# Decayed cumulative sum of a matrix product: group 14 by seven block products instead of eight, slots 34 to 243 ordered by a list scheduler

## The chip, the cores and the metric

The kernel runs on one core of a Trainium2 chip. The metric is the device time of one execution in microseconds (us); three executions of the kernel before gave a median of 905.18 us (904.9 to 905.23). The engines are named as in the profile: PE (TensorE, matmuls), PEld (its weight loads), DVE (VectorE), ACT (ScalarE), POOL (GpSimd) and SP (SyncE, which here only issues DMAs).

## The reference

```python
B, S, D = x.shape                 # 16, 2048, 1024, float32
xw = x @ w                        # w: 1024 x 1024
out[:, 0, :] = xw[:, 0, :]
for t in range(1, S):
    out[:, t, :] = decay[None, :] * out[:, t - 1, :] + xw[:, t, :]
```

A product of a 32768 x 1024 matrix with a 1024 x 1024 one, and behind it, in each of the 16 batches and 1024 columns, a first-order recurrence along 2048 time steps.

## The kernel before, in words

**Data.** Time is cut into 64 chunks of 512 steps; four chunks make a batch and two neighbouring chunks a group (31 whole groups, 0 to 30, and chunks 62 and 63 one by one at the end). x comes by DMAs from POOL's queue that turn fp32 into bf16 (`load`, "L", four to a chunk, ring `xb` of 3). DVE transposes the chunk in 32 x 32 blocks (`turn`, "T", ring `xw` of 2), ACT copies it in two halves into the form that the matmul reads (`part`, "X" and "Y", 128 x 2048 bf16 each, ring `xt` of 5). w lies in SBUF as bf16 (`wsb`).

**Slots.** A slot is one tile: a group (1024 time steps) times 128 output columns n of 8. `slots` lists them group by group: 248 slots with two chunks, then 16 with one chunk. PE works a slot as 16 matmuls 128 x 128 x 512 (8 blocks k of the contraction times 2 chunks) into one PSUM tile `ps`, from a ring of three (two PSUM banks each, called a slot's bank below); the last slots take `spare` too. Slot 112 is the first of group 14, slot 244 is the fifth of group 30.

**The recurrence of a tile** (class `Tile`) goes in one of two ways. *Alone*: DVE scans all 1024 steps from PSUM (`S`, `run`, line 228). *Paired*, which halves the scan: ACT copies `ps` to SBUF (`copy`, "p", line 185) and multiplies the steps of one parity by the decay (`odd`, "g", line 170, into a buffer `h` of four); `zero` ("z") sets the element before the first; POOL adds them (`join`, "j", line 205); DVE scans the 512 pair sums with the squared decay (`S`, line 210); ACT multiplies the results by the decay (`even`, "h"), and POOL adds that to the other parity (`fill`, "c", line 253). `save` ("k") keeps the last step for the next group of the batch. In the slots in question every fourth tile (n % 4 == 3) is alone and the rest is paired. The copy lies in `xs` (ring of 3), the result in `so` (ring of 4).

**Leaving.** DVE transposes the tile into `ot` (`back`, "B", line 265, ring of 4); four tiles fill one `ot` (a lump), and SP's queue stores it with four DMAs (line 289).

**Order.** Each engine takes its instructions in program order. The order is written by hand as letters and slots in `agenda` for slots 0 to 33 and the last 20; for the slots between, `usual` and `later` give the same pattern in each group (two tables of lead slots say when T, X and Y of a chunk come). In the tail (`agenda` -20 and on), flips change which tiles are alone.

Of the kernel before, what the change touches and what calls it, by code (L numbers as in the profile page):

```python
# [25 lines left out]
def kernel(  # L26
# [41 lines left out]
    CR = CH // NQ  # L68

# [24 lines left out]
    def ot_tile(nj):  # L94
        return ring(sb, "ot", 4, [128, nj, CR])

# [22 lines left out]
    def part(c, copy, m0, m1, j0=0, j1=NJ):  # L119
        if c not in xt_of:  # L120
            xt_of[c] = ring(sb, "xt", 5, [128, M, 2, TL], BF16)
        src = xw_of[c][:, m0:m1, j0:j1].rearrange("p m j i e -> p m e (j i)")
        pin(copy(out=xt_of[c][:, m0:m1, :, j0 * P:j1 * P], in_=src))  # L123
# [17 lines left out]
    class Tile:  # L141
# [3 lines left out]
        def __init__(self, g, n, ps, outlets):  # L145
            self.b, self.t0 = chunks[g[0]]
            self.T = TL * len(g)
            self.n, self.ps, self.outlets = n, ps, outlets
            self.paired = n % R != R - 1
            if len(tiles) in flips or len(tiles) - len(slots) in flips:  # L150
                self.paired = not self.paired
            self.turn = len(tiles)
            self.lot = sum(t.paired for t in tiles)
            self.prev = None if self.t0 == 0 else last[n]
            if self.t0 + self.T < S:
                last[n] = const.tile([128, 1], FP32, name=f"keep{n}", bufs=2)
                self.keep = last[n]
            else:
                self.keep = None

        @property
        def so(self):
            if not hasattr(self, "held"):
                self.held = sb.tile([128, 2 * TL + 2], FP32, name=f"so{self.turn % 4}")
            return self.held

        def decayed(self, src, h=None):
            if h is None:
                h = ring(sb, "h", 4, [128, TL])[:, 0:self.T // 2]
            pin(nc.scalar.activation(  # L170
                out=h, in_=src, func=mybir.ActivationFunctionType.Copy,
                scale=dec[:, self.n:self.n + 1]))
            return h
# [8 lines left out]
        def copy(self):  # L182
            self.xs = sb.tile([128, 2 * TL], FP32, name=f"xs{self.lot % 3}")[:, 0:self.T]
            for t, ps in self.parts():
                pin(nc.scalar.copy(out=self.xs[:, t:t + ps.shape[1]], in_=ps))  # L185

        def odd(self):
            self.g = ring(sb, "h", 4, [128, TL])[:, 0:self.T // 2]
            for t, ps in self.parts():
                size = ps.shape[1]  # L190
                self.decayed(ps[:, 0:size:2], self.g[:, t // 2:(t + size) // 2])

# [3 lines left out]

        def zero(self):
            if self.prev is None:
                pin(nc.gpsimd.memset(self.so[:, 1:2], 0.0))  # L199
            else:  # L200
                pin(nc.scalar.copy(out=self.so[:, 1:2], in_=self.prev))  # L201

        def join(self):
            odds = self.xs[:, 1:self.T:2]
            pin(nc.gpsimd.tensor_tensor(out=odds, in0=self.g, in1=odds, op=ALU.add))  # L205

        def scan(self):
            T, n, so = self.T, self.n, self.so
            if self.paired:
                pin(nc.vector.tensor_tensor_scan(  # L210
                    out=so[:, 3:T + 2:2],
                    data0=squares[-1][:, n:n + 1].to_broadcast([128, T // 2]),
                    data1=self.xs[:, 1:T:2],
                    initial=0.0 if self.prev is None else self.prev,
                    op0=ALU.mult,
                    op1=ALU.add,
                ))
            else:
                for t, ps in self.parts():
                    self.run(ps, t, ps.shape[1])  # L220

        def run(self, ps, t, size):
            n, so = self.n, self.so
            if t:
                before = so[:, t + 1:t + 2]
            else:
                before = 0.0 if self.prev is None else self.prev
# [13 lines left out]
        def complete(self):  # L241
            if self.paired:
                self.even()
                self.fill()
            if self.keep is not None:
                self.save()

        def even(self):
            self.h = self.decayed(self.so[:, 1:self.T + 1:2])

        def fill(self):
            T = self.T
            pin(nc.gpsimd.tensor_tensor(  # L253
                out=self.so[:, 2:T + 2:2], in0=self.h, in1=self.xs[:, 0:T:2], op=ALU.add))

        def save(self):
            pin(nc.scalar.copy(out=self.keep, in_=self.so[:, self.T + 1:self.T + 2]))  # L257
# [15 lines left out]
    class Outlet:  # L273


        def __init__(self, ns, nj, half=0, queues=(nc.sync,), pieces=1):
# [3 lines left out]
            self.ot = ot_tile(nj)  # L280
# [135 lines left out]
    def turn_and_load(c):  # L416
# [61 lines left out]
        21: "p20 g20 L S18 X8 j20 B17 B19",  # L478
        22: "L h18 p21 c18 B16 k18 g21 B18 Y8 z20 L j21 S20",
        23: "p22 z21 z22 S21 L h20 g22 T9 c20 h21",  # L480
        24: "k21 k20 j22 S23 X9 L c21 Y9 B20 L",
        25: "B23 k23 p24 B21 g24 z24 j24 S22 z25",
        26: "p25 T10 k22 h22 g25 c22 S24 X10 j25",
        27: "B22 p26 S25 g26 z26 Y10 j26",
# [28 lines left out]
    later = {}  # L513
    begun = {"T": 12, "X": 11, "Y": 11}
    for c in range(5, nch):
        first = c // 2 * K
        ahead = (7, 6, 4) if c % 2 else (11, 10, 8)
        for letter, a in zip("TXY", ahead):
            if c >= begun[letter]:
                later.setdefault(first - a, []).append(f"{letter}{c}")  # L520

    def usual(s):
        paired = [t.paired for t in tiles]
        do = [f"P{s}"] if paired[s] else []
        if paired[s - 1]:
            do.append(f"S{s - 1}")
        if not paired[s]:
            do.append(f"S{s}")
        do.append(f"C{s - 1}")
        if paired[s - 2]:  # L530
            do.append(f"B{s - 2}")
        if not paired[s - 1]:
            do.append(f"B{s - 1}")
        return do + later.get(s, []) + ["L"] * (2 if len(loads) > NQ else 1)

    def rest(s):
        do = [f"S{s - 1}"] if tiles[s - 1].paired else []
        do.append(f"C{s - 1}")
        if tiles[s - 2].paired:
            do.append(f"B{s - 2}")  # L540
        return do + [f"B{s - 1}"] + later.get(s, []) + ["L"] * len(loads)

# [3 lines left out]

    perform(agenda[-99].split())
    spares = [spare] + [ring(psp, "spare1", 1, [128, TL])]
    for step, (g, n) in enumerate(slots):
        T = TL * len(g)  # L550
        left = step - len(slots)
        if n % R == 0:
            ns, nj = range(n, n + R), T // P
            outlets = [Outlet(ns, nj)]
# [54 lines left out]
        do = agenda.get(step, agenda.get(left) if left >= -20 else None)  # L609
        if do is None:  # L610
            do = usual(step)
        else:
            do = do.split()
            if left == -20:
                do = rest(step) + do
        perform(do)
# [29 lines left out]
```

## Time and profile before

| What | Value |
|---|---|
| median of three runs | 905.18 us (904.9 to 905.23) |
| profiled execution, its own time | 905.68 us |
| span of the profiled execution | 903.9 us |
| granted TensorE clock, mean | 0.999 |
| DMA, mean | 227 GB/s |
| store of `ot`, issue to landing, median | 10.9 us |
| load of `xb`, issue to landing, median | 7.9 us |

The profile is of one execution. Rows of groups give a line, an engine and an operation, the tile written and the tiles read, then the count, the busy time, the mean length of one in ns, and the idle time of that engine just before them with what ended it. A length holds the pipeline's fill, so back to back the operations start somewhat closer together than their length. In a timeline a row gives start and length in us. In the chain of waits a row gives start and length of a piece.

### The profile page before, as it was taken

Reading aid. Unit: us, or ns where it says so; the run is one execution under the profiler, and the core shown is the slowest. Engines: PE = TensorE matmul, PEld = TensorE weight load, DVE = VectorE, ACT = ScalarE, POOL = GpSimd, SP = SyncE. Lnnn points to the kernel's source line nnn. Section 1 sums busy time; section 2 is a strip of 40 time slices with the busy share of each in tenths; the row PEclk is TensorE's granted clock in tenths of the full one; section 3 lists DMA queues with packets and bytes.
Section 4 is the critical chain, followed back from the end, with each engine's and each line's share of the span. In section 5 each row is a group of like instructions: output and inputs, shape, how many; then the busy total and the mean of one; then the engine's idle time right before and its main releaser. Section 6 shows DMA issues by size and latency. Waiting matters only on the chain.

```text
span 903.9 us, 12113 instructions
## 1 busy us (share of the span) xinstructions
PE 896.4 (99%) x4217; PEld 412.7 (46%) x4217; DVE 825.5 (91%) x628; ACT 686.3 (76%) x957; POOL 656.7 (73%) x755
## 2 busy tenths in 40 slices
PE   8999999999999999999999999999999999999997
PEld 5544444444444444444444444444444444444444
DVE  4999998999999999999998999999999999999997
ACT  4899967777877877877778778778777787787742
POOL 7978678777767768677677677777777776776632
PEclk9999999999999999999999999999999999999999
DMA  9999999999999999999999999999999999999868
GB/s 186 190 215 215 226 256 217 215 237 236 254 242 260 243 251 257 248 237 226 224 237 229 224 229 229 230 224 229 231 227 228 233 232 222 226 233 211 176 143 235
DMA packets 402542, 204.77 MB, mean 227 GB/s; under 512 B 8752, under 2 KB 401456, under 8 KB 402480
## 3 DMA queue, kind: packets, MB, share of 16 engines
q1 hardware_dynamic: 265168, 134.76, 61.0%
q0 software_dynamic: 137024, 68.70, 56.6%
q8 instruction: 33, 0.54, 0.2%
q10 hardware_dynamic: 288, 0.52, 0.2%
q14 instruction: 29, 0.24, 0.1%
HBM read 138.42 MB, written 134.22 MB: 302 GB/s over the span
## 4 chain that ended last, share of the span: by engine, by line
PE 97%; DMA 1%; POOL 0%; issue 0%; DVE 0%; DVEq 0%; POOLq 0%
PE ps L131 96%; DMA xb<-in_x_dram 1%; PE spare L131 1%; POOL xb L105 0%; PE spare L395 0%; PE ps L395 0%; DVE h L399 0%; DVE xw L115 0%; DVEq L115 0%; POOLq L630 0%
## 5 line engine op out<-in xcount | busy, mean ns | idle before, releaser
L131 PE MATMUL ps<-xt,wsb 128*128 128x512 bf16 (+1 forms) x4028 | 866.3, 378 | 0.0
L131 PEld LDWEIGHTS <-wsb 128*128 128x128 bf16 x4168 | 407.5, 98 | 478.0 <-ACT wsb L313 0.8
L205 POOL TENSOR_TENSOR xs<-h,xs 128x512 f32<-128x512 f32 (+1 forms) x190 | 242.8, 1278 | 188.1 <-ACT h L170 85.3
L185 ACT COPY xs<-ps 128x1024 f32<-128x1024 f32 (+1 forms) x190 | 188.9, 994 | 152.9 <-PE ps L131 148.1
L265 DVE STREAM_TRANSPOSE ot<-so 128x1024 f32<-128x1024 f32 (+1 forms) x260 | 300.0, 1191 | 2.1 <-POOL so L199 1.1
L253 POOL TENSOR_TENSOR so<-h,xs 128x512 f32<-128x512 f32 (+1 forms) x190 | 241.0, 1270 | 43.7 <-ACT h L170 27.8
L123 ACT COPY xt<-xw 128x2048 bf16<-128x2048 bf16 (+3 forms) x136 | 242.3, 1790 | 8.7 <-DVE xw L115 8.7
L105 POOL DMA_DIRECT2D xb<-in_x_dram x264 | 174.0, 660 | 5.6 <-DMA xb<-in_x_dram 3.2
L170 ACT ACTIVATE h<-so,dec 128x512 f32<-128x512 f32 (+1 forms) x190 | 145.3, 766 | 28.7 <-DVE so L210 25.2
L115 DVE STREAM_TRANSPOSE xw<-xb 128x2048 f32<-128x2048 f32 (+3 forms) x78 | 147.4, 1901 | 8.0 <-DMA xb<-in_x_dram 7.9
L210 DVE TENSOR_TENSOR_SCAN so<-spare,keep,xs 128x512 f32<-128x512 f32 (+1 forms) x97 | 119.9, 1239 | 26.7 <-POOL xs L205 26.4
L210 DVE TENSOR_TENSOR_SCAN so<-spare,xs 128x512 f32<-128x512 f32 x93 | 113.3, 1219 | 27.4 <-POOL xs L205 24.5
L170 ACT ACTIVATE h<-ps,dec 128x512 f32<-128x512 f32 (+1 forms) x190 | 130.0, 684 | 0.0
L228 DVE TENSOR_TENSOR_SCAN so<-dec,ps 128x1024 f32<-128x1024 f32 x34 | 76.8, 2260 | 1.0 <-ACT h L170 1.0
L228 DVE TENSOR_TENSOR_SCAN so<-dec,keep,ps 128x1024 f32<-128x1024 f32 (+1 forms) x35 | 75.9, 2168 | 0.2 <-issue 0.2
L257 ACT COPY keep<-so 128x1 f32<-128x1 f32 x136 | 25.3, 188 | 9.5 <-DVE so L228 9.0
L201 ACT COPY so<-keep 128x1 f32<-128x1 f32 x97 | 18.4, 191 | 2.7 <-DVE ot L265 2.4
L131 PE MATMUL spare<-xt,wsb 128*128 128x512 bf16 (+3 forms) x60 | 12.6, 329 | 0.0
L131 PE MATMUL ps<-xw,wsb 128*128 128x256 bf16 (+3 forms) x68 | 11.2, 301 | 0.4 <-DVE xw L115 0.4
L199 POOL MEMSET so<- 128x1 f32 x93 | 10.7, 117 | 0.6 <-DVE ot L265 0.6
L331 PE MATMUL spare<-idle 128*128 128x512 bf16 x22 | 6.8, 479 | 1.2 <-DVE idle L321 1.2
L306 POOL DMA_DIRECT2D ot<-in_w_dram x12 | 6.6, 552 | 1.7 <-DMA xb<-in_x_dram 0.8
(39 smaller groups left out, 37.9 us busy)
## 6 DMA issues: line engine op xcount, KB each, us to landing
out_dram<-ot SPq DMA_DIRECT2D x248, 512.0 KB, 10.9
xb<-in_x_dram POOLq DMA_DIRECT2D x248, 256.0 KB, 7.9
out_dram<-ot SPq DMA_DIRECT2D x12, 256.0 KB, 4.2
ot<-in_w_dram POOLq DMA_DIRECT2D x12, 128.0 KB, 5.6
xb<-in_x_dram POOLq DMA_DIRECT2D x8, 128.0 KB, 5.4
out_dram<-xb SPq DMA_DIRECT2D x3, 256.0 KB
xb<-in_x_dram POOLq DMA_DIRECT2D x4, 144.0 KB, 7.0
ot<-in_w_dram ACTq DMA_DIRECT2D x2, 256.0 KB, 5.2
```

The source lines that it names most:

```text
L105: pin(nc.gpsimd.dma_start(out=xb_of[c][quad(q), j0:j1], in_=_ap(x, [[D, P], [P * D, j1 - j0], [1, CQ]], (b * S + t0 + j0 * P) * D + q * CQ)))
L115: pin(nc.vector.transpose(out=dst.rearrange("p (m j i) -> p j m i", m=M, i=P)[:, j0:j1, m0:m1], in_=src.rearrange("p (j m c) -> p j m c", ...
L123: pin(copy(out=xt_of[c][:, m0:m1, :, j0 * P:j1 * P], in_=src))
L131: pin(nc.tensor.matmul(out=ps[:, t0:t1] if ps.shape[1] >= t1 else ps, lhsT=lhs, rhs=rhs, start=(k == 0 and t0 == start), stop=(stop and k ...
L170: pin(nc.scalar.activation(out=h, in_=src, func=mybir.ActivationFunctionType.Copy, scale=dec[:, self.n:self.n + 1]))
L185: pin(nc.scalar.copy(out=self.xs[:, t:t + ps.shape[1]], in_=ps))
L205: pin(nc.gpsimd.tensor_tensor(out=odds, in0=self.g, in1=odds, op=ALU.add))
L210: pin(nc.vector.tensor_tensor_scan(out=so[:, 3:T + 2:2], data0=squares[-1][:, n:n + 1].to_broadcast([128, T // 2]), data1=self.xs[:, 1:T:2 ...
L228: pin(nc.vector.tensor_tensor_scan(out=so[:, t + 2:t + 2 + size], data0=dec[:, n:n + 1].to_broadcast([128, size]), data1=ps, initial=befor ...
L253: pin(nc.gpsimd.tensor_tensor(out=self.so[:, 2:T + 2:2], in0=self.h, in1=self.xs[:, 0:T:2], op=ALU.add))
L257: pin(nc.scalar.copy(out=self.keep, in_=self.so[:, self.T + 1:self.T + 2]))
L265: pin(nc.vector.transpose(out=outlet.ot[:, :, c0:c0 + P], in_=self.so[:, 2 + t0:2 + t0 + nj * P].rearrange("p (i t) -> p i t", t=P)))
```

## The change

What it does, part by part:

1. **Group 14 by block products.** The two chunks a and b of group 14, split in halves of the contraction, and the weights of two neighbouring column tiles, split in the same halves, are 2 x 2 blocks. The product is formed in the Strassen-Winograd manner: DVE adds halves of x four times (`sums`, 128 x 2048 bf16 each, three into a new tile `sx`, one in place in b's `xt`); POOL forms 20 differences of weight blocks once (`differ`, 128 x 512 bf16, into a new tile `wd`); and for each of the four pairs of column tiles seven products of four matmuls each (`product`, names a1, a2, b1, c, a3, b2, a4) are summed in two halves of one `ps` tile and in `spare0`. ACT copies partial sums out between products (`lift`, 128 x 512, four to a pair), and DVE adds or subtracts the rest into the result lines (`join` inside `mixed_pair`, 128 x 512 from PSUM, three to a pair).
2. **Slots 34 to 243 in the orders of a list scheduler.** `steady` makes a `Job` for every step of these slots (a quarter of a slot's matmuls, a copy, a scan, a load and so on) with an engine, a duration from `cost`, a key (about when it is due) and the jobs it waits for. `in_order` runs them through at these durations: an engine that is free takes the ready job with the lowest key. The program is then written in the order in which they started. [...]
3. **Which tiles are alone.** Of the slots 34 to 243 outside group 14, a share of 0.1 (0.06 in groups 13, 15 and 16) is scanned alone: slots 44, 54, 64, 74, 84, 94, 104, 128, 141, 151, ..., 231, 241, 19 in all. All others, and the whole of group 14, are paired. Before, 53 were alone.
4. **Buffers.** `xs` goes; the paired tile is copied into `so` and worked on in place, with a ring of 7 for `so`. The rings of `ot` and `xt` go from 4 to 3 and from 5 to 4. `ot` and the kept last step are taken when first written.
5. **Loads** in these slots are issued one slot apart, with a lead that the scheduler keeps.
6. In slots 20 to 27 the hand-written X and Y of chunks 8 to 10 move back by one to three slots (those of 10 into the scheduled part), to fit the smaller ring of `xt`.

The diff, cut to its core:

```diff
+    OTS, XTS, SOS, HS = 3, 4, 7, 4
+    FROM, TO = 34, 244
+    SUMS, SUMT = ('dve', 'dve', 'dve', 'dve'), -24
+    WBY, WLEAD, WSTEP = "pool", 120, 4
+    SHARE = {-1: 0.06, 0: 0, 1: 0.06, 2: 0.06, 3: 0.1, 9: 0.1}
+    merged = (14,)
...
-            xt_of[c] = ring(sb, "xt", 5, [128, M, 2, TL], BF16)
+            xt_of[c] = ring(sb, "xt", XTS, [128, M, 2, TL], BF16)
...
         def copy(self):
-            self.xs = sb.tile([128, 2 * TL], FP32, name=f"xs{self.lot % 3}")[:, 0:self.T]
             for t, ps in self.parts():
-                pin(nc.scalar.copy(out=self.xs[:, t:t + ps.shape[1]], in_=ps))
+                pin(nc.scalar.copy(out=self.line[:, t:t + ps.shape[1]], in_=ps))
...
-        21: "p20 g20 L S18 X8 j20 B17 B19",
-        22: "L h18 p21 c18 B16 k18 g21 B18 Y8 z20 L j21 S20",
+        21: "p20 g20 L S18 j20 B17 B19",
+        22: "L h18 p21 c18 B16 k18 g21 B18 z20 L j21 S20",
         23: "p22 z21 z22 S21 L h20 g22 T9 c20 h21",
-        24: "k21 k20 j22 S23 X9 L c21 Y9 B20 L",
-        25: "B23 k23 p24 B21 g24 z24 j24 S22 z25",
-        26: "p25 T10 k22 h22 g25 c22 S24 X10 j25",
-        27: "B22 p26 S25 g26 z26 Y10 j26",
+        24: "X8 k21 k20 j22 S23 Y8 L c21 B20 L",
+        25: "B23 k23 p24 B21 g24 z24 j24 S22 X9 z25",
+        26: "p25 T10 k22 h22 g25 c22 Y9 S24 j25",
+        27: "B22 p26 S25 g26 z26 j26",
...
+    cost = {"p": .91, "g": .6, "z": .12, "j": 1.27, "S": 1.16, "D": 2.2, "h": .68, "c": 1.27,
+            "k": .11, "B": 1.14, "T": 1.14, "X": 1.79, "L": .66, "half": .5, "both": .62,
+            "sum": 1.2, "wpool": 1.15, "wdve": .65, "slow": 4.2}
+    each = R * PASS
...
+        for s in range(FROM, len(slots)):
+            c = slots[s][0][0]
+            starts.setdefault(c // 2, t)
+            if s < TO:
+                t += (7 if c // 2 in merged else 8) * 2 * PASS
+        for i in range(5 * R if merged else 0):
+            weights.append(Job(WBY, cost["w" + WBY], starts[min(merged)] - WLEAD + WSTEP * i,
+                               lambda i=i: differ(i % 5, i // 5)))
...
+        def chunk(c):
+            need = starts[c // 2] - 18 + (c % 2) * 8
...
+                    a.early = max(4.0, need - 3 * 4 * each * R + 2) + q * each * R
...
+                    turned[c] = Job(
+                        "dve", cost["T"], need + 2 * half,
...
+                        ends + [turned.get(c - 1), part_of.get((c - 2, 1)), turned.get(c)])
...
+                    part_of[c, half] = Job(
+                        "act", cost["X"], need + 3 + 3 * half,
...
+                        [turned[c], part_of.get((c - 1, half))] + used.get(c - XTS, []))
...
+        def normal(s, t):
...
+                        tile.ps = psp.tile([128, 2 * TL], FP32, name=f"ps{bank % 3}")
+                    for k in (2 * q, 2 * q + 1):
+                        for i in range(2):
+                            matmul(tile.ps[:, i * TL:(i + 1) * TL], n, k, xt_of[g[i]])
...
+        def product(out, xs, ws, begin):
+            for k in range(R):
+                pin(nc.tensor.matmul(out=out, lhsT=ws(k), rhs=xs[:, k // 2, k % 2],
+                                     start=begin and k == 0, stop=k == R - 1,
+                                     skip_group_check=True))
...
+            a1 = mult("a1", done + weights + (after_ps[bank - 3] if bank >= 3 else []))
+            A1 = lift(0, 1, "a", at("a1"), [a1, gone[0]])
+            a2 = mult("a2", [A1])
+            A2 = lift(0, 0, "a", at("a2"), [a2, gone[0]])
+            b1 = mult("b1", [a1])
+            B1 = lift(1, 0, "b", at("b1"), [b1, gone[1]])
+            c = mult("c", [after_spare[0], part_of[c1, 1]])
+            C = join(0, 1, "c", ALU.add, at("c"), [c, A1])
+            a3 = mult("a3", [A2])
+            A3 = join(1, 0, "a", ALU.subtract, at("a3"), [a3, B1])
+            b2 = mult("b2", [B1])
+            B2 = join(0, 0, "b", ALU.subtract, at("b2"), [b2, A2], True)
+            a4 = mult("a4", [A3])
+            A4 = lift(1, 1, "a", at("a4"), [a4, gone[1]])
...
+        order = in_order()
+        for job in order:
+            job.do()
```

Of the jobs' keys the prediction uses these: a paired tile's p is due when its matmuls end, S 3.5 us and B 8 us after that; a sum 24 us ahead of group 14; an X 15, 12, 7 and 4 us ahead of its group's start in `starts`.

## The prediction

> **What bounds the kernel now.** I read the page's busy shares first, then the chain that ended last in order of time, then the busy time of the engines around group 14 and in the tail, then single rows for prices, and last the timeline of the tail.
>
> ```profile
> span 903.9 us, 12113 instructions
> PE 896.4 (99%) x4217; PEld 412.7 (46%) x4217; DVE 825.5 (91%) x628; ACT 686.3 (76%) x957; POOL 656.7 (73%) x755
> ...
> 43.64 830.69 PE ps L131 x3848
> ```
>
> PE is busy 99% of the span, and from 43.6 us on the chain is matmuls alone: 830.69 us for 3848 of them is 0.2159 us each, with no gap. So only fewer matmuls, or a new gap between them, can move the time. A slot (16 matmuls) takes 3.454 us. Counting back from the end, slot 112 (the first of group 14) starts at about 399.3 us and slot 244 at about 855.2 us.
>
> ```profile
> 372.00:399.60 27.60, 27.60 (x130) 12.52 (x129) 25.47 (x19) 21.48 (x31) 20.08 (x21) 1.00 1.21 242
> 399.60:427.20 27.60, 27.60 (x130) 12.48 (x129) 25.52 (x19) 21.49 (x29) 20.97 (x27) 1.00 1.19 229
> ```
>
> These windows are groups 13 and 14 (columns: PE, PEld, DVE, ACT, POOL busy us, then granted clock, DMA). PE has no idle time, DVE is at 92%, ACT at 78%, POOL at 73 to 76%. The clock is 1.00.
>
> ```profile
> L265 DVE STREAM_TRANSPOSE ot<-so 128x1024 f32<-128x1024 f32 x248 | 292.4, 1216 | 2.1 <-POOL so L199 1.1 <-POOL so L253 0.4
> L205 POOL TENSOR_TENSOR xs<-h,xs 128x512 f32<-128x512 f32 x183 | 237.6, 1298 | 177.5 <-ACT h L170 79.9 <-issue 53.8 <-ACT so L201 39.1
> L123 ACT COPY xt<-xw 128x2048 bf16<-128x2048 bf16 x124 | 235.7, 1904 | 3.0 <-DVE xw L115 3.0
> L210 DVE TENSOR_TENSOR_SCAN so<-spare,xs 128x512 f32<-128x512 f32 x93 | 113.3, 1219 | 27.4 <-POOL xs L205 24.5
> L228 DVE TENSOR_TENSOR_SCAN so<-dec,ps 128x1024 f32<-128x1024 f32 x34 | 76.8, 2260 | 1.0 <-ACT h L170 1.0
> L399 DVE COPY xb<-ps 128x512 f32<-128x512 f32 x1 | 0.7, 692 | 0.0
> ```
>
> These are the prices. From the timeline, start to start on a full engine: copy p 0.91, g 0.58, h 0.69, X 1.84 us on ACT; j and c 1.25 on POOL; paired S 1.2, B 1.16, whole T 2.25 on DVE.
>
> ```profile
> 858.25 3.47 DVE L265 STREAM_TRANSPOSE ot<-so 128x1024 f32<-128x1024 f32 x3
> 862.71 2.29 DVE L228 TENSOR_TENSOR_SCAN so<-dec,ps 128x1024 f32<-128x1024 f32 x1 [0.98 <-ACT h L170]
> 893.42 1.28 DVE L228 TENSOR_TENSOR_SCAN so<-dec,keep,ps 128x512 f32<-128x512 f32 x1 [0.18 <-issue]
> ```
>
> In the tail DVE has no idle between 862.71 (scan of slot 245, 7.5 us after slot 244 began) and 893.42, where it waits 0.18 us. There DVE is as tight as PE: a later start than 862.71, counted from slot 244, passes to the end but for 0.2 us.
>
> **Removed.** A normal group is 8 x 16 = 128 matmuls. Group 14 becomes 4 pairs x 7 products x 4 matmuls = 112 of the same form. 16 x 0.2159 = **-3.45 us**, all on the path. Outside the group no matmul goes or comes.
>
> **Other engines in slots 34 to 243.** Tiles scanned alone fall from 53 to 19. Each one that becomes paired takes 1.0 us from DVE and gives 2.18 us to ACT and 2.5 us to POOL. By the prices a normal slot of 3.454 us then has ACT 0.9 x 2.18 + 4 x 1.84 / 8 + 0.1 = 2.98 (86%), POOL 0.9 x 2.5 + 0.66 + 0.05 = 2.96 (86%), DVE 0.9 x 1.2 + 0.1 x 2.2 + 1.16 + 0.56 = 3.02 (87%). None is a bound. The cover is that a slot's PSUM bank is wanted only two slots (6.9 us) after the slot ends, of which p and g take 1.5 us. The orders come from durations that match these rows within 0.1 us, so I charge **+0.2** for misfits (0 to 2). If the cover were gone, each such lag would stop PE one for one.
>
> **Loads and rings.** xb loads stand one slot apart on POOL's queue and land in 7.9 us (the median), against some 18 us from the last load to its turn's due time: nothing. SP's stores follow the transposes as before; an ot buffer comes round after two further lumps (27.6 us), against 10.9 us of landing: nothing. The hand-moved X8 to X10 wait for slot 23's end with the ring of four xt; they still end some four slots before use: nothing. Slots 0 to 33 keep their matmuls.
>
> **Weight differences.** 20 POOL operations on 512 elements, nearest row 1.30 us: 26 us. They wait for nothing, so the scheduler puts them into POOL's idle 0.49 us a slot; the 78 slots ahead have 38 us. Nothing, unless the operation costs over 1.9 us.
>
> **Sums.** Four DVE additions on 2048 bf16 elements, not shown in this trace. Lower bound from the DVE bf16 copies of 448 and 576 elements (355 and 418 ns): 0.49 ns an element, 1.13 us each. Upper bound from the transposes of 1024 and 2048 (1216 and 2285 ns): 2.29 us. I take 1.2, nearest to the bf16 rows: 4.8 us in all (4.5 to 9.2). They need all four X of group 14, which, with four xt buffers, can't begin before group 12 ends, 27.6 us ahead. ACT then has about 1.3 us a slot left from p, g, h and z, so an X fits every 1.4 slots: the last ends some 9 us before the group, the sums near its start. The first product needs the first sum; product c needs none and covers 0.86 us.
> **Inside group 14.** In 24.2 us DVE has 12 additions from PSUM (row: the 512-element PSUM copy, 0.69) = 8.3, 8 S = 9.7, 8 B = 9.3, T = 4.5, so 32 us without the sums. From 5 us ahead of the group to its end (29.2 us) some 9.4 slots' S and B fall due: 4.8 + 8.3 + 9.4 x 2.36 + 4.5 = 39.8, a lag of 10.6 us, made up at 0.43 us a slot over some three groups. What covers it: seven `so` lines. A normal tile's line is free some 9 us after its slot and wanted again after 24, so 12 to 15 us of lag are hidden; inside the group only 5.8 us (slot 119 wants the line of slot 112). There PE has other products and the next slots' matmuls in its order. Waits of a2 to a4 for ACT's 0.59 us lifts are filled by the neighbouring pair. I charge **+0.3** (0 to 4).
>
> **Tail.** Two things in the code. First, 78 + 4 + 124 = 206 PSUM tiles leave the ring of three shifted: slot 244 takes the bank of slot 242, not of 241. Second, the due times of chunks 62 and 63 are set as if their group started at slot 244 instead of 248, so ACT runs four X in the 13.8 us after slot 239 frees their buffers: 4 x 1.84 + three p and g (239, 240, 242; 241 is alone) 4.5 + three h 2.1 + small copies 0.3 = 14.2 us. Bank 242 is free about 0.7 us after slot 244 should start. Then p and g of slot 243, and from its p to its B 6.5 us (382.32 to 388.83 in the trace for such a chain) plus 1.16: B243 ends about 8.4 us after slot 244's due start. Slot 245's scan stands behind it on DVE, against 7.5 before: 0.9 - 0.2 = 0.7 on DVE, and 0.7 on PE, side by side. **+0.7** (0.2 without any lag on ACT; 2.5 if it lags by one X more).
>
> **Sum.** The profiled execution took 905.68 us (1.78 beyond its span), 0.5 above the median 905.18. 905.68 - 3.45 + 0.2 + 0.3 + 0.7 = 903.4, which is **902.9 us** as a median.
>
> **Rivals.**
> *Nothing is lost* (0.12). The tail's lag is absorbed: 905.18 - 3.45 = 901.7. Against it: the full DVE in the tail.
> *The sums come late* (0.10). In the trace the last X of group 14 begins at 398.39 and ends 1.0 us after the group's start; placed so, the first product waits 1.0 + 1.2 + 0.2, less 0.86 for c, and the third sum comes 2.4 us after the first, of which products cover 1.7: about 2.2 us in all, 905.1. For it: all four X must be done, where before the last was wanted 1.7 us into the group. Against it: ACT's 1.3 us a slot.
> *The sums hold POOL too* (0.08). If POOL stands still for their 4.8 us, joins wait, the four h buffers stay taken, g waits for one, and a bank is given back late; with an X (1.84) ahead of g that is 4.8 + 1.84 against a cover of 6.9 - 1.5 = 5.4: 1.2 us, 904.1. For it: POOL at 86%. Against it: in this trace DVE's and POOL's operations run side by side (380.61 and 381.94 us, at their usual length), though none of DVE's reads two large SBUF operands. [...]
> *DVE sets the pace in group 14* (0.28), the slower side. It decides once DVE lags by over 5.8 us at the middle of the group and PE has nothing else in order: 10.6 - 5.8 = 4.8 us in place of 0.3, 907.4; with sums of 2.29 us it is 4.4 more, 911.8. For it: 32 us of work in 24.2. Against it: lines and banks that hide 12 us around it.
> *The forecast* has 0.42, by itself 902.1 to 904.5.
>
> [...]
>
> About 0.2%, 1.8 us, is what a measurement can tell from no change: faster is below 903.4, slower above 907.0. Faster: 0.12 + 0.33 of the forecast = 0.45. Same: 0.09 of the forecast, 0.10 of the late sums, 0.08 of the held POOL, 0.02 of the last = 0.29. Slower: 0.26. The range, 901.7 to 907.5, takes in the first three rivals and the nearer end of the last.
>
> **What would show it.** Right: some 16 fewer 512-column matmuls; PE idle near 1 us between slot 34 and the tail; PE waiting for ACT about 0.7 us where slot 244 starts (near 852 us); DVE's scan of slot 245 about 8.4 us behind it; four new DVE additions of about 1.2 us ending near 399 us. Wrong: PE idle of several us at or after 399 us waiting for DVE, additions over 2 us, PE gaps all through the ordered slots, or a granted clock below 1.00 behind a gap.

## The result, and the profile after

| | Median | Executions |
|---|---|---|
| before | 905.20 us | 904.90 to 905.29 (4) |
| after | 915.13 us | 914.31 to 916.63 (4) |

The change makes the kernel slower: the ratio is 1.0112, 95% interval 1.0099 to 1.0124, or 9.9 us. The forecast was 902.9 us with a range of 901.7 to 907.5. The profiled execution after took 915.48 us and its span is 913.7 us, 9.8 us more than the span before; the traces are compared by their spans.

The busy shares come first (the page after, its first part, and two of its rows of groups: tile written and tile read, count, then busy us and mean ns, then the idle time ahead of them).

```profile
span 913.7 us, 12192 instructions
PE 897.0 (98%) x4201; PEld 411.6 (45%) x4201; DVE 804.9 (88%) x696; ACT 753.5 (82%) x1083; POOL 767.5 (84%) x860
...
L138 PE MATMUL ps<-xt,wsb 128*128 128x512 bf16 (+1 forms) x3900 | 841.1, 378 | 5.4 <-ACT h L184 5.4
L619 POOL TENSOR_TENSOR wd<-wsb 128x512 bf16<-128x512 bf16 x20 | 23.2, 1164 | 0.1
```

PE has 4201 matmuls where it had 4217: the 16 are gone, as forecast. DVE has less to do than before (88% against 91%), and no engine but PE is near a bound. Still PE's busy time did not fall by 3.45 us; it rose from 896.4 to 897.0 us, and idle time came on top. So the loss is in gaps and in slower matmuls. PE's timeline from the first ordered slots on shows the places (start, length, operation, count, and in brackets the idle time before with what ended it; where no idle time stands, a row begins up to 0.17 us before the one above it ends, since matmuls overlap).

```profile
59.66 80.02 PE L138 MATMUL ps<-xt,wsb 128*128 128x512 bf16 x370
141.90 7.07 PE L138 MATMUL ps<-xt,wsb 128*128 128x512 bf16 x32 [2.22 <-ACT h L184]
152.11 253.68 PE L138 MATMUL ps<-xt,wsb 128*128 128x512 bf16 x1168 [3.15 <-ACT h L184]
405.63 1.89 PE L751 MATMUL ps<-sx,wsb 128*128 128x512 bf16 x8
407.36 1.03 PE L751 MATMUL spare<-xt,wd 128*128 128x512 bf16 x4
411.02 1.86 PE L751 MATMUL ps<-sx,wd 128*128 128x512 bf16 x4 [2.63 <-ACT so L827]
412.68 1.91 PE L751 MATMUL ps<-sx,wsb 128*128 128x512 bf16 x4
...
424.02 1.02 PE L751 MATMUL ps<-sx,wd 128*128 128x512 bf16 x4 [0.78 <-ACT so L827]
...
438.47 1.02 PE L751 MATMUL ps<-xt,wd 128*128 128x512 bf16 x4 [1.10 <-DVE so L833]
439.33 445.01 PE L138 MATMUL ps<-xt,wsb 128*128 128x512 bf16 x2060
```

There are five gaps and no others: two some 10 and 20 us after the ordered part begins (slot 34 starts at 129.16 us), three in group 14. From 439.33 us on, PE runs 445 us without a stop, through the ordered slots behind group 14 and through the whole tail. The matmuls of four at 411.02 and 412.68 start 1.66 and 1.70 us apart, 0.42 us each instead of 0.216: half speed. The granted clock says the same (windows: length, then PE, PEld, DVE, ACT, POOL busy, then granted clock, DMA share, GB/s).

```profile
130.00:160.00 30.00, 24.63 (x107) 10.64 (x106) 16.86 (x15) 24.35 (x33) 29.19 (x35) 0.94 1.10 211
400.00:420.00 20.00, 17.37 (x73) 7.44 (x72) 17.88 (x18) 13.38 (x20) 14.48 (x15) 0.91 0.69 140
440.00:860.00 420.00, 420.00 (x1948) 190.38 (x1947) 376.68 (x312) 369.68 (x517) 362.79 (x396) 1.00 1.20 232
```

In 130 to 160 us the clock lacks 0.06 of 30 us, in 400 to 420 us 0.09 of 20 us, 1.8 us each time: a stretch of 3.41 us at half clock with each of the gaps of 3.15 and 2.63 us. The first stretch begins 0.5 us before the matmuls do, so 2.9 us of it fall on matmuls (up to 155.04 us); of the second, all. With them the account closes within 0.2 us:

| | us |
|---|---|
| 16 matmuls fewer | -3.45 |
| start of the ordered part: idle 2.22 + 3.15 | +5.4 |
| group 14: idle 2.63 + 0.78 + 1.10 | +4.5 |
| matmuls at half clock for 2.9 and 3.4 us, half of each lost | +3.2 |
| matmuls don't overlap across the five gaps, 0.379 - 0.216 each | +0.8 |
| the matmuls began earlier (46.28 us against 47.10) | -0.8 |
| sum (spans: +9.8) | +9.7 |

POOL shows something else at 130 to 160 us: 29.19 of 30 us busy, where its slot was worked out at 86%.

### The profile page after: what moved, and what is told of

Read it like the earlier page. It is cut to its first block, busy times and chain, and to the rows that moved or that the text cites. A ratio compares the mean times of both kernels' runs of the same rounds, so it can differ in the third digit from the quotient of the medians.

```text
span 913.7 us, 12192 instructions
## 1 busy us (share of the span) xinstructions
PE 897.0 (98%) x4201; PEld 411.6 (45%) x4201; DVE 804.9 (88%) x696; ACT 753.5 (82%) x1083; POOL 767.5 (84%) x860
## 4 chain that ended last, share of the span: by engine, by line
PE 77%; DVE 7%; ACT 4%; POOL 2%; issue 2%; DVEq 0%; ACTq 0%; POOLq 0%
PE ps L138 75%; DVE ot L276 2%; DVE so L221 2%; ACT h L184 2%; PE ps L751 1%; ACT xt L130 1%; DVE xw L122 1%; POOL so L216 1%; PE spare L138 1%; POOL wd L619 1%; ACT so L202 1%; POOL so L264 1%; DVE sx L768 0%; DVE so L239 0%; ACT so L827 0%
## 5 line engine op out<-in xcount | busy, mean ns | idle before, releaser
L138 PE MATMUL ps<-xt,wsb 128*128 128x512 bf16 (+1 forms) x3900 | 841.1, 378 | 5.4 <-ACT h L184 5.4
L264 POOL TENSOR_TENSOR so<-h,so 128x512 f32<-128x512 f32 (+1 forms) x224 | 288.2, 1289 | 88.8 <-ACT h L184 66.5
L216 POOL TENSOR_TENSOR so<-h,so 128x512 f32<-128x512 f32 (+1 forms) x224 | 289.7, 1295 | 42.6 <-ACT h L184 32.1
L202 ACT COPY so<-ps 128x1024 f32<-128x1024 f32 (+1 forms) x216 | 216.5, 1002 | 63.5 <-PE ps L138 62.8
L184 ACT ACTIVATE h<-so,dec 128x512 f32<-128x512 f32 (+1 forms) x233 | 179.5, 773 | 56.9 <-DVE so L221 54.8
L122 DVE STREAM_TRANSPOSE xw<-xb 128x1024 f32<-128x1024 f32 (+4 forms) x130 | 153.5, 1193 | 6.9 <-DMA xb<-in_x_dram 6.9
L184 ACT ACTIVATE h<-ps,dec 128x512 f32<-128x512 f32 (+1 forms) x215 | 148.9, 693 | 0.4 <-POOL so L210 0.4
L221 DVE TENSOR_TENSOR_SCAN so<-spare,so 128x512 f32<-128x512 f32 x110 | 131.5, 1202 | 15.6 <-POOL so L216 13.0
L221 DVE TENSOR_TENSOR_SCAN so<-spare,keep,so 128x512 f32<-128x512 f32 (+1 forms) x114 | 139.3, 1226 | 6.4 <-POOL so L216 5.7
L239 DVE TENSOR_TENSOR_SCAN so<-dec,ps 128x1024 f32<-128x1024 f32 x17 | 38.3, 2259 | 0.7 <-PE ps L138 0.6
L239 DVE TENSOR_TENSOR_SCAN so<-dec,keep,ps 128x1024 f32<-128x1024 f32 (+1 forms) x18 | 36.4, 2022 | 1.5 <-PE ps L138 1.3
L619 POOL TENSOR_TENSOR wd<-wsb 128x512 bf16<-128x512 bf16 x20 | 23.2, 1164 | 0.1
```

The lines of the kernel that those rows point to most:

```text
L122: pin(nc.vector.transpose(out=dst.rearrange("p (m j i) -> p j m i", m=M, i=P)[:, j0:j1, m0:m1], in_=src.rearrange("p (j m c) -> p j m c", ...
L138: pin(nc.tensor.matmul(out=ps[:, t0:t1] if ps.shape[1] >= t1 else ps, lhsT=lhs, rhs=rhs, start=(k == 0 and t0 == start), stop=(stop and k ...
L184: pin(nc.scalar.activation(out=h, in_=src, func=mybir.ActivationFunctionType.Copy, scale=dec[:, self.n:self.n + 1]))
L202: pin(nc.scalar.copy(out=self.line[:, t:t + ps.shape[1]], in_=ps))
L221: pin(nc.vector.tensor_tensor_scan(out=so[:, 3:T + 2:2], data0=squares[-1][:, n:n + 1].to_broadcast([128, T // 2]), data1=so[:, 3:T + 2:2] ...
L239: pin(nc.vector.tensor_tensor_scan(out=so[:, t + 2:t + 2 + size], data0=dec[:, n:n + 1].to_broadcast([128, size]), data1=ps, initial=befor ...
```

## The experiments

The account leaves two losses to explain: at the start of the ordered part (6.9 us with its clock; the forecasts below reckon 7.1) and in group 14 (6.2). Where the kernels have an interval, it is of the ratio to the kernel before, run beside it on the same chip (904.94 to 905.25 us; e1 to e8 ran on one chip, e9 to e12 on another). A trace is of one execution, and not always of the median one (e2: 909.49 us against 911.16; e7: 914.92 against 913.26). Two executions can differ in their gaps without any cause in the program: up to the tail e1 and e7 have the same order on every engine, and the start has gaps of 2.04 and 0.98 us in the one trace, and a single one of 2.31 us with half clock in the other.

The theories at first: **A**, the scheduler's plan begins with idle engines at slot 34, while the real ones still carry the hand-written slots' work, so its orders are optimistic there; **B**, the weight differences overfill POOL there; **D**, the sums in group 14, which run beside POOL's operations, take longer than the 1.2 us for which the planner keeps both DVE and POOL, and the lifts come late. Its rival **E**, in the forecasts of e4 to e6, says that DVE has too much work in group 14 whatever the sums take. The rows that D starts from are these (after, DVE's timeline at the sums, and POOL's below it):

```profile
392.79 1.20 DVE L768 TENSOR_TENSOR sx<-xt 128x2048 bf16<-128x2048 bf16 x1
394.02 4.44 DVE L768 TENSOR_TENSOR sx<-xt,sx 128x2048 bf16<-128x2048 bf16 x2
398.39 2.31 DVE L768 TENSOR_TENSOR xt<-xt,xt 128x2048 bf16<-128x2048 bf16 x1
```

```profile
395.11 2.28 POOL L216 TENSOR_TENSOR so<-h,so 128x512 f32<-128x512 f32 x1
397.34 2.28 POOL L264 TENSOR_TENSOR so<-h,so 128x512 f32<-128x512 f32 x1
```

The first sum takes 1.20 us, the three behind it 2.2 us each, and POOL's additions, 1.30 us elsewhere, take 2.28. The starts alternate, 1.05 to 1.18 us apart (DVE 394.02, POOL 395.11, DVE 396.26, POOL 397.34, DVE 398.39, POOL 399.57); as read here, the two engines take turns, and each one's row holds the wait for the other. The sums end at 400.70 us, 7.9 us after they began, not 4.8.

**e1: no products at all.** Group 14 is computed as the other groups, so no weight differences, no sums, 16 matmuls more; the rest of the change stays.

```diff
-    merged = (14,)
+    merged = ()
```

> No group is formed by block products: all 210 slots keep 16 matmuls, and the weight differences go too. The scheduler, its buffers and its loads stay. Theory A (the plan begins with idle engines at slot 34, while ACT, DVE and POOL are really some 4 us behind there): the two PE gaps at about 140 and 149 us and the half-clock stretch behind them, 7.1 us in all, stay; 905.2 + 7.1 = 912.3. Theory B (the POOL operations for weight differences, 6 of them planned in the first 13 us, push joins back and so make these gaps): the gaps go, 905.2. Either way no gap near 400 us.

Measured: 915.64 us, ratio 1.0120 (1.0105 to 1.0136), as slow as the whole change. The start's gaps shrink but stay, and nothing runs at half clock there (its PE timeline):

```profile
142.09 7.07 PE L138 MATMUL ps<-xt,wsb 128*128 128x512 bf16 x32 [2.04 <-ACT h L184]
150.14 701.18 PE L138 MATMUL ps<-xt,wsb 128*128 128x512 bf16 x3248 [0.98 <-ACT h L184]
...
878.72 1.89 PE L138 MATMUL ps<-xt,wsb 128*128 128x512 bf16 x8 [2.33 <-DVE so L239]
```

So the first gap is not the weights' doing, the second largely is. The tail brought a loss that no theory had: 5.3 us in six gaps, the largest the 2.33 us above. Without group 14 the alone tiles fall on other slots (slot 241 is paired here), and the four X that the tail runs in one stretch crowd ACT. That may be the tail mechanism of the prediction; e7 tests it.

**e2: the weight differences later**, none planned before 60 us of the ordered part.

```diff
             weights.append(Job(WBY, cost["w" + WBY], ...
+            weights[-1].early = 60.0
```

> As after, but no weight difference may be planned before 60 us into the scheduled part. Theory A: the gaps at 140 and 149 us stay, 914 to 915. Theory B: they go, and with them the half clock behind them: 915.1 - 7.1 = 908.0. The gaps in group 14 (6.2 us with their half clock) stay either way.

Measured: 911.16 us, 1.0074 (1.0056 to 1.0092). Start gaps 2.68 and 0.98 us and no half clock: B is right for the second gap (3.15 to 0.98) and for the clock behind it, and wrong for the first. The order in group 14 came out differently as well (four gaps of 0.5 to 0.9 us and no half clock), so only part of the 4.0 us gained belongs to the start. The trace is of the fastest execution; two of the four took 912.6 and 912.8 us.

**e3: the plan starts late.** The scheduler's ACT, DVE and POOL are busy for their first 3.5, 4.5 and 5.0 us.

```diff
+        for e, late in (("act", 3.5), ("dve", 4.5), ("pool", 5.0)):
+            idle[e] = late
+            events.append((late, -10 ** 6 - len(events), None))
```

> As after, but the scheduler's plan begins with ACT, DVE and POOL busy until 3.5, 4.5 and 5.0 us, where the trace of after has them when slot 34 starts on PE. Theory A: the order then fits what is there, the gaps at 140 and 149 us go: 915.1 - 7.1 = 908.0, and group 14 keeps its gaps. Theory B: little changes, 914 to 915, since the differences still fill POOL's first 20 us.

Measured: 910.37 us, 1.0059 (1.0044 to 1.0074). The start's two gaps fall from 5.4 us to 0.58 + 0.39 us, without half clock, though the weights still lie there; one of 0.45 us comes at 68 us, before the ordered part. Group 14 kept its gaps (3.24, 0.78 and 1.10 us). An order that allows for the work in hand takes most of the start's loss; it does not say what makes that work late.

**e4: copies in place of the sums.** Group 14's values are not the products; matmuls, order and tiles are the same.

```diff
-                pin(engine.tensor_tensor(out=flat(out), in0=flat(one), in1=flat(two), op=ALU.add))
+                pin(engine.tensor_copy(out=flat(out), in_=flat(one if i < 3 else two)))
```

> As after, in the same order, but each of the four sums on DVE is a plain copy of one operand (so group 14's values are not the products). Theory D (the sums take 7.9 us beside POOL instead of the planned 4.8; so the scans behind them, then the h's on ACT, then the first lifts are late and PE waits): copies of about 0.7 us end 5 us sooner, the 2.6 us gap at 408 us and the half clock behind it (1.7) go: 915.1 - 4.3 = 910.8, and of the two later gaps (0.8 and 1.1) some may go too. Theory E (DVE has 32 us of work in 24 us of group 14 whatever the sums take): gaps of 4 us in the group stay, in later places; 914 or more.

Measured: 911.53 us, 1.0076 (1.0061 to 1.0091). In group 14 the first gap falls from 2.63 to 0.30 us and the half clock there goes; 0.78 and 1.10 stay. The start's first gap is 1.2 us shorter in this trace too (1.04 for 2.22), with nothing changed there, so not all of the 3.6 us gained is the sums'.

```profile
405.07 1.89 PE L751 MATMUL ps<-sx,wsb 128*128 128x512 bf16 x8
406.80 1.03 PE L751 MATMUL spare<-xt,wd 128*128 128x512 bf16 x4
408.12 1.02 PE L751 MATMUL ps<-sx,wd 128*128 128x512 bf16 x4 [0.30 <-ACT so L827]
```

That is what D said. How sums that end 5 us ahead of the group can stop its third product is in ACT's timeline of after:

```profile
405.37 0.78 ACT L184 ACTIVATE h<-so,dec 128x512 f32<-128x512 f32 x1 [1.98 <-DVE so L221]
...
407.67 0.77 ACT L184 ACTIVATE h<-so,dec 128x512 f32<-128x512 f32 x1 [0.86 <-DVE so L221]
...
409.91 1.05 ACT L827 COPY so<-ps 128x512 f32<-128x512 f32 x2
```

The first product starts at 405.63 us without a wait. But DVE, which the sums held 3.1 us longer than planned, is late with the scans of the slots before (L221). ACT takes its instructions in program order, waits for those scans with the multiplications that stand ahead (L184), and reaches the first two lifts (L827) only at 409.91 us. PE's a2 waits for the lift.

Two repairs were tried next, alone and with others: a plan that knows the true length of the sums, and the tail's due times.

**e5: late start, and the planner told that a sum takes 2.0 us.**

```diff
+        for e, late in (("act", 3.5), ("dve", 4.5), ("pool", 5.0)):
+            idle[e] = late
+            events.append((late, -10 ** 6 - len(events), None))
...
-            "sum": 1.2, ...
+            "sum": 2.0, ...
```

> As e3_late_start (910.4), and the scheduler plans each sum at 2.0 us, the mean that the trace of after shows for the four, instead of 1.2. Theory D (the plan, not the work, is what fails at group 14's start): lifts stand where their data is ready, the 3.2 us gap and the half clock behind it (1.7) go: 910.4 - 4.9 = 905.5, and the gaps of 0.8 and 1.1 us may go too, down to 903.6. Theory E (DVE's 32 us of work in 24): the gap moves to a later product, 909 to 911.

Measured: 911.35 us, 1.0062 (1.0042 to 1.0082). Group 14's gaps are 0.48, 0.19 and 1.19 us and no half clock is left, but the trace has 15 gaps now, 8.1 us in all, up to 1.30 us, between 140 and 645 us. E had the time nearly right (909 to 911) but not the place: the group lost 1.9 us. What the two repairs gave is lost again elsewhere.

**e6: e5, and the weight differences after 60 us as in e2.** To the diff of e5 comes the line of e2:

```diff
             weights.append(Job(WBY, cost["w" + WBY], ...
+            weights[-1].early = 60.0
```

> As e5, and no weight difference before 60 us into the scheduled part. By theories A and D with B for the second gap of the start: the start loses under 0.5 us, group 14 1 to 2 us: 905.0 - 3.45 + 0.5 + 1.5 = 903.6. If the products can't be had without 4 us of gaps (theory E), 906 or more.

Measured: 917.88 us, 1.0127 (1.0090 to 1.0164), with executions from 912.48 to 919.81. The profile is of the execution of 912.48 us and has 12 gaps, 8.75 us, the largest 1.95 us at 190.7; group 14 has 2.0 us of them. Why other executions of the same program took 5 to 7 us more, no trace shows.

**e7: no products, and the tail's due times mended** (chunks 62 and 63 get the time of slot 248).

```diff
-    merged = (14,)
+    merged = ()
...
-            if s < TO:
+            if s < TO + 4:
```

> As e1_no_products (915.6), but the due times of chunks 62 and 63 are counted from their own group, four slots after slot 244. The tail theory of the prediction (four X placed 13.8 us early make ACT late, so banks are late and DVE enters the tail late): the gaps from 852 to 881 us (4.7 us) and the 0.6 before the end go, 915.6 - 5.3 = 910.3; the start's 3.0 us stay. Rival (the tail suffers because slot 243 is paired and its transpose stands ahead of slot 245's scan): the gaps stay, 915.

Measured: 913.26 us, 1.0087 (1.0071 to 1.0103). Of e1's six gaps in the tail one is left, 2.16 us, with a half clock behind it; the start had one of 2.31 us, also with half clock. So the due times are behind 3.2 of the 5.3 us of gaps, but with the half clock only 2.4 us came back (medians), not the 5.3 forecast. What made the rest, the rival of the forecast or something else, no run here separates.

**e8: only the true length of the sums**, without the late start.

```diff
-            "sum": 1.2, ...
+            "sum": 2.0, ...
```

> As after (915.1), only with the sums planned at 2.0 us. Theory D: the start keeps its 7.1 us, group 14 loses its first gap and half clock (4.3): 910.8. If the late ACT at group 14's start comes from the start's lag, carried through the 70 slots between, nothing changes: 914 to 915.

Measured: 914.76 us, 1.0097 (1.0079 to 1.0115), 4 us over what D says. D's own gap is gone: group 14 has 0.30, 0.19 and 1.19 us and no half clock, 4.5 us better than after. The start kept its gaps (1.82 and 3.14 us, this time without half clock). But five new gaps, 3.9 us, stand between 459 and 620 us. What they may go with is in DVE's timeline, 21 us ahead of the largest (1.44 us at 513.0):

```profile
491.43 1.25 DVE L276 STREAM_TRANSPOSE ot<-so 128x1024 f32<-128x1024 f32 x1 [3.31 <-DMA out_dram<-ot]
```

A transpose, the first of a lump, stands 3.3 us, until the store of the lump three before has landed. That led to **F**: with three `ot` buffers, stores that land late hold DVE, and through it the rest. The prediction had dismissed this. The landings in the traces are these: one DMA lands 10.9 us (median) after its issue before and 9.6 us in after, but from the first issue of a lump to the fourth SP's queue takes 4.5 us before and 7.0 in after (medians), and the last one lands 16.6 us after the lump's last transpose before and 21.4 us in after (medians over the 31 lumps with landings recorded; longest 43.1 and 32.5 us). In the long cases SP comes late to the lump at all: before, the one complete at 171.3 us is first issued at 192.2. The planner counts 13 us. Four kernels test F.

**e9: e1 with four buffers `ot`.** Without the products there is room for the fourth in SBUF, as this run shows; the whole change, with `sx` and `wd`, was not tried with a ring of four. Every engine's instructions stand in the order of e1.

```diff
-    OTS, XTS, SOS, HS = 3, 4, 7, 4
+    OTS, XTS, SOS, HS = 4, 4, 7, 4
...
-    merged = (14,)
+    merged = ()
```

> As e1_no_products (915.6), with the ring of ot back at 4 (there is room, since the products' tiles are gone). Theory F (with three ot buffers a transpose waits for a store that takes 21 us in the middle and up to 30, against the planned 13; DVE stands 3 us at about 99 us, and ACT and POOL behind it are late when the scheduled part begins): DVE's stand at 99 us goes and with it the start's gaps (3.0 us); 912.3, with the tail's 5.3 us left. Theory A alone (the plan starts with idle engines): the start keeps 2 to 3 us, 915.

Measured: 911.96 us, 1.0080 (1.0065 to 1.0095), against 912.3 by F, and 3.7 us below e1. The start has no gap left; the first gap of PE in the ordered part comes in the tail, whose gaps are e1's:

```profile
46.83 801.47 PE L138 MATMUL ps<-xt,wsb 128*128 128x512 bf16 x3712
849.00 7.07 PE L138 MATMUL ps<-xt,wsb 128*128 128x512 bf16 x32 [0.71 <-ACT h L184]
```

And the place where the store bites shows at 99 us, 30 us ahead of the ordered slots. DVE's timelines there, e1 and then e9:

```profile
96.69 2.25 DVE L239 TENSOR_TENSOR_SCAN so<-dec,ps 128x1024 f32<-128x1024 f32 x1
102.18 3.50 DVE L276 STREAM_TRANSPOSE ot<-so 128x1024 f32<-128x1024 f32 x3 [3.25 <-DMA out_dram<-ot]
```

```profile
96.89 2.24 DVE L239 TENSOR_TENSOR_SCAN so<-dec,ps 128x1024 f32<-128x1024 f32 x1
99.06 3.46 DVE L276 STREAM_TRANSPOSE ot<-so 128x1024 f32<-128x1024 f32 x3
```

In the hand-written slots DVE stands 3.25 us for a store, and its lag is carried into slot 34. (In the trace of after the same stand reads `[3.38 <-POOL so L216]`. But it ends at 102.0 us, and the lump complete at 70.8 us lands at 101.9, 31.1 us later: it is the store there too.) One short stand for a store is left in e9, 1.4 us at 153 us, and PE has no gap behind it.

**e10: the kernel before with three buffers `ot`**, nothing else.

```diff
-        return ring(sb, "ot", 4, [128, nj, CR])
+        return ring(sb, "ot", 3, [128, nj, CR])
```

> The kernel before, with the ring of ot at 3 instead of 4 and nothing else changed. Theory F in its strong form (the smaller ring alone costs): DVE waits for stores, 3 us at about 99 us and now and then later, and with DVE at 92% PE waits too: 907 to 910. In its weak form (the ring only bites where the order has no slack): DVE waits, PE hardly, 905.2 to 906.

Measured: 913.96 us, 1.0097 (1.0078 to 1.0116): one buffer less costs the kernel before 8.7 us, more than F said. PE in its timeline, then DVE in its own, then the row of waits (us in total, times, longest):

```profile
191.47 691.10 PE L131 MATMUL ps<-xt,wsb 128*128 128x512 bf16 x3192 [5.24 <-DVE so L228]
```

```profile
102.33 3.50 DVE L265 STREAM_TRANSPOSE ot<-so 128x1024 f32<-128x1024 f32 x3 [2.45 <-DMA out_dram<-ot]
186.77 1.25 DVE L265 STREAM_TRANSPOSE ot<-so 128x1024 f32<-128x1024 f32 x1 [6.64 <-DMA out_dram<-ot]
```

```profile
DVE ot L265 <- DMA out_dram<-ot: 12.8, 5, 6.6
```

DVE stands 6.64 us for a store, and PE behind it 5.24 us, with 6.83 us at half clock around it, of which 4.1 us fall on matmuls. With a gap of 0.26 us at 172 us and 0.3 for the overlap of matmuls lost at the two gaps that is 0.26 + 5.24 + 2.0 + 0.3 = 7.8 us, of the 8.1 by which the span rose.

**e11: the change with half of its stores**; half of the output is not written.

```diff
-                for i, q in enumerate((0, 2, 1, 3)):
+                for i, q in enumerate((0, 2)):
```

> As after (915.1), but only two of a lump's four stores are issued, so half of the output is not written. Stores then land in about half the time. Theory F: the start's gaps (5.4 us and 1.7 of half clock) go or halve, 908 to 911; group 14 keeps its 6.2 us. Theory A alone: the start's gaps stay, 914 to 915.

Measured: 911.53 us, 1.0072 (1.0057 to 1.0087). No transpose waits for a store. Of the start's two gaps the first is gone; one of 2.12 us is left at 149 us, where POOL has the weight differences, without half clock. Group 14 has its three gaps and its half clock. The time is 0.5 us above the range that F gave.

**e12: e11 with e3's late start and e5's length of the sums.** The ring's wait, the plan's idle start and the short sums are out; half of the output is not written.

```diff
-                for i, q in enumerate((0, 2, 1, 3)):
+                for i, q in enumerate((0, 2)):
...
+        for e, late in (("act", 3.5), ("dve", 4.5), ("pool", 5.0)):
+            idle[e] = late
+            events.append((late, -10 ** 6 - len(events), None))
...
-            "sum": 1.2, ...
+            "sum": 2.0, ...
```

> As e5_true_sums (911.4: plan with the late start and sums of 2.0 us), with only two of a lump's four stores, half of the output not written. If the scattered gaps of 0.2 to 1.3 us that e5 shows from 150 to 650 us, and its spread of 4.5 us between executions, come from stores that hold up the transposes (F), they go: 903.9, products' own gaps of 1.9 us left; and executions agree within 0.5 us. If they come from orders that have no slack for anything, they stay: 909 or more.

Measured: 905.14 us, 0.9999 (0.9990 to 1.0009), over ten executions of 904.76 to 905.74. PE, with all its gaps ahead of the last slots:

```profile
59.78 339.24 PE L138 MATMUL ps<-xt,wsb 128*128 128x512 bf16 x1571
...
401.91 1.02 PE L754 MATMUL ps<-sx,wd 128*128 128x512 bf16 x4 [0.30 <-ACT so L830]
...
406.58 1.02 PE L754 MATMUL ps<-sx,wd 128*128 128x512 bf16 x4 [0.19 <-ACT so L830]
...
415.02 1.02 PE L754 MATMUL ps<-xt,wd 128*128 128x512 bf16 x4 [1.19 <-DVE so L836]
...
453.94 419.82 PE L138 MATMUL ps<-xt,wsb 128*128 128x512 bf16 x1943 [0.48 <-ACT xt L130]
```

The start is clean, and the scattered gaps of e5, which differs from e12 only in the stores, are gone but for one of 0.48 us that waits for an X (e5 has it too): the others came from the stores. Fewer stores also let the loads land sooner (6.7 us for 9.8, medians), but that isn't it, as this row of e5's waits shows (us in total, times, longest):

```profile
DVE ot L276 <- DMA out_dram<-ot: 24.8, 9, 5.9
```

From 60 us on DVE stood for a load once in e5, for 0.3 us, and e12 has neither kind of stand there. What is left is 2.16 us of idle time in four gaps, and 0.6 us for the overlap of matmuls lost there: 2.8 of the 3.45 us that the products save. Forecast for this kernel was 903.9 us, so it took 1.2 us more than F says; three of the four gaps lie inside the products' own group. A kernel with all repairs and its whole output was not run.

## Why the prediction was wrong

**The term that failed first: the ring of `ot`.** "an ot buffer comes round after two further lumps (27.6 us), against 10.9 us of landing: nothing". The 10.9 us are the page's row for a single DMA. A lump leaves by four, issued one after another from a queue that can itself be late, and the last one lands 16.6 us after the lump is ready in the kernel before and up to 43.1; after the change 21.4 and up to 32.5. A ring of three covers 27.6 us, less when DVE's transposes come early; before, with four buffers, no transpose waited for a store. e9 shows it at the start (four buffers, same order: no gap), e10 by itself (8.7 us), e12 against e5 in the slots after.

**Misfits of the orders: charged at 0.2 us (0 to 2), measured 6.9 at the start.** "The orders come from durations that match these rows within 0.1 us" was read as if durations were all that a plan holds. It also holds a beginning (idle engines, where DVE and ACT came in late: e3) and landing times (13 us, where the medians are 16.6 and 21.4). The 20 weight differences cost 1.16 us each, less than the 1.30 priced, and are hidden on average; but they were planned into POOL's free time in the very slots where the lag from the store had to be made up (e2, e11), so most of the second gap is theirs.

**The sums: taken at 4.8 us in all, measured 7.9.** That lies inside the 4.5 to 9.2 that the prediction allowed, but its forecast went by 4.8. That the sums hold POOL was a rival at 0.08, priced at 1.2 us. In the trace of after each delays the other: the first sum, beside a POOL addition in its last 0.2 us alone, takes 1.20 us, the three whose starts alternate with POOL's take 2.2 to 2.31, and POOL's additions there 2.28, against 1.30 elsewhere. The rival followed the delay from POOL through the `h` buffers to the PSUM banks. It went another way: DVE 3.1 us late, its scans late, ACT waiting in order behind them, the lifts late (e4). So **inside group 14** "I charge +0.3 (0 to 4)" became 4.5 us of idle time, of which 2.3 us and a half clock are the sums' and 2.2 the products' own.

**The clock was named as a sign of error and had no term.** The two stretches cost 1.5 and 1.7 us, and 3.2 in all are a third of the loss.

**The slower rival had the side, and its price for group 14 only by luck.** "DVE sets the pace" put 4.8 us, and 907.4 us in all, on a DVE that is full in group 14; the idle time there was 4.5. But DVE had slack there: between 415 and 432 us it stood 4.0 us itself, waiting for PE and ACT, and in e12 the same DVE work in the group goes with 1.7 us of idle PE. What counts is when DVE comes to its work, not how full it is. The rival of late sums did not happen: they ended at 400.70 us, and the first product began at 405.63 without a wait.

**The tail: charged at 0.7 us, cost next to nothing.** PE gets slot 244's bank 0.07 us late, and DVE scans slot 245 7.6 us behind the start of slot 244 (before 7.5, forecast 8.4):

```profile
872.79 2.25 DVE L239 TENSOR_TENSOR_SCAN so<-dec,ps 128x1024 f32<-128x1024 f32 x1
```

In after slot 241 is scanned alone, which spares ACT a copy there. Where it is paired (e1), the tail lost 5.3 us in gaps rather than 0.7, and e7 puts some 3 of them on the due times.

**Right:** the 16 matmuls and their 3.45 us, PE as the only bound on average, DVE's additions in group 14 (0.64 to 0.69 us, priced 0.69), and the sum without POOL beside it (1.20 us, priced 1.2).

Open: why e6's executions differ by 7 us, and why SP's queue falls as far behind as it does. The second bears on why one buffer costs e10 more than the start of the changed kernel loses: e10 stands at 187 us for the store of a lump that took 39.3 us to land, where the lumps of the changed kernel around that time took some 21.

## What to carry to other kernels

A ring that feeds stores is sized by the time from the last write into a buffer until the last DMA of that buffer has landed, and by its longest (43.1 us before, 32.5 after), not by the median of one DMA (10.9 and 9.6). Where engines take work in program order, an order written out from a plan is as good as the plan's start and its landing times, and a gap in PE is to be followed back through each engine's queue, sometimes 30 us, before it is put down to the operation that ended it. When an algorithm saves 3.45 us of a busy engine, ask first what room its new tiles and orders take from the buffers that kept it busy.

## What the runs showed of the hardware

- **Half clock with short gaps.** Idle gaps of 2.16 and 2.31 (both e7), 2.63 (after, e11), 3.14 (e4), 3.15 (after) and 3.24 us (e3) each went with 3.41 us at half clock (granted 0.50), up to 1.7 us lost; gaps of 2.04 (e1), 2.12 (e11), 2.22 (after), 2.32 (e9), 2.33 (e1), 2.68 (e2) and 3.14 us (e8) did not. The length of a gap alone doesn't decide. The 2.63 us gap in e11 was followed by slow matmuls only 0.9 us later. In the two rows below the first window is of after, behind 3.15 us, the second of e8, behind 3.14 (the clock stands before the last two columns):

```profile
152.11:155.04 2.93, 2.93 (x7) 0.98 (x7) 2.56 (x3) 1.52 (x3) 2.93 (x6) 0.50 1.19 221
152.20:156.00 3.80, 3.77 (x18) 1.76 (x18) 3.41 (x3) 2.39 (x5) 3.80 (x6) 1.00 1.27 242
```

- **SP's queue issues faster with fewer stores.** With four stores to a lump, SP's first and last issue lie 4.5 us (before) and 7.0 us (after) apart in the median; with two (e12) they lie 0.4 us apart, and the last one lands 8.4 us after the lump is ready, at most 14.2.
- **Copies are longer beside POOL too.** In e4 two of the four bf16 copies of 2048 elements took 0.67 and 0.69 us, and two, beside POOL, 1.78; POOL's additions beside them took 1.74 and 1.75 us.
- **The spread goes with the stores.** Ten executions of e12 spread over 1.0 us, and thirteen of before beside them over 0.8; five of e5, the same program as e12 with all its stores, over 4.5, with seven of before beside them over 1.5.
